# Row sums on one core: the first block loaded in one piece instead of four, and SyncE made to see the loads' ends before the store

## The chip, the cores and the metric

One core of one Trainium2 chip. VectorE (DVE) and ScalarE (ACT) do the sums; SyncE (SP in the views) issues every transfer, and 16 DMA engines carry it out in packets (before's records have 896 packets of 64 KB, 56 one behind the other on each of 16 engines). The metric is the device time of one execution in microseconds (us), lower is better. Every run quoted here is of the fast state, with a granted clock of 1.0. One kernel's executions differ by up to 0.7 us among themselves. Apart from one experiment (e3), the effects studied here are no larger than that, so times are compared within one set of runs on one chip, and the parts are read from traces, where most of them repeat far more closely.

## The reference

```python
x = np.random.randn(32, 512, 1024).astype(np.float32)      # 67.11 MB
out = (np.sum(x, axis=-1) * 0.5).astype(np.float32)         # 32 x 512
```

The 16,384 rows lie on 128 partitions, 128 rows each. They are worked in eight blocks of 16 rows per partition (8.39 MB a block).

## The kernel before

Seven whole blocks, then one cut in pieces. Three buffers; DVE sums one half of a block, ACT the other.

```python
for b in range(n_blocks - 1):
    t = x_pool.tile([P, B, D], fp32, name="xb")             # 3 buffers
    step = 4 if b == 0 else 1                               # block 0: four loads of 32 partitions,
    for q in range(step):                                   # every fourth partition each
        nc.sync.dma_start(out=t[q:P:step], in_=x_rows[q:P:step, c0 : c0 + B, :])
    # ... reduce_sum and a multiply on DVE for rows 0-7, act_row on ACT for rows 8-15
# last block: three loads of whole rows (8, 5, 2), two for the last row (640 and 384 columns)
# ... the last two DVE sums take the last row's two parts
nc.sync.dma_start(out=out_view, in_=res)                    # the store

def start_loads_at_entry(nc_):
    # moves SyncE's leading loads, up to the first that has to wait, in front of the entry barrier
    ...
```

Block 0's four loads are called strided quarters below. So before has 4 + 6 + 5 = 15 loads. The first six need no buffer to come free and are issued in front of the entry barrier, the point at which all engines wait for each other at the start. Each DMA counts on one of eight semaphores, which the program hands out in turn. The store is the 16th DMA and gets the eighth semaphore. At the end of the program SyncE waits once more for every semaphore and then enters the final barrier.

Of the kernel before, what the change touches and what calls it, by code (L numbers as in the profile page):

```python
# [1 line left out]

# [4 lines left out]


@with_exitstack
def kernel(  # L10
    ctx: ExitStack,
    tc: tile.TileContext,
    x: bass.AP,
    multiplier: float,
    out: bass.AP,
):







    nc = tc.nc
    P = nc.NUM_PARTITIONS
    fp32 = mybir.dt.float32
    ADD = mybir.AluOpType.add

    x_flat = x.flatten_outer_dims()
    N, D = x_flat.shape  # L30
    rows = N // P
    x_rows = x_flat.rearrange("(p c) d -> p c d", p=P)
    out_view = out.rearrange("b s -> (b s)").rearrange("(p c) -> p c", p=P)
    mul = float(multiplier)

    B = 16
    n_blocks = rows // B
    assert N == P * rows and rows == n_blocks * B

    x_pool = ctx.enter_context(tc.tile_pool(name="x", bufs=3))  # L40
    res_pool = ctx.enter_context(tc.tile_pool(name="res", bufs=1))
    sums = res_pool.tile([P, rows], fp32, name="sums")
    res = res_pool.tile([P, rows], fp32, name="res")
    part = res_pool.tile([P, 1], fp32, name="part")

    def act_row(t, r, col):
        nc.scalar.activation(  # L47
            out=t[:, r, :],
            in_=t[:, r, :],
            func=mybir.ActivationFunctionType.Copy,  # L50
            scale=mul,
            accum_out=res[:, col : col + 1],
        )

    def dve_span(t, r, lo, hi, dst, start=0.0):
        mid = (lo + hi) // 2
        nc.vector.tensor_tensor_reduce(  # L57
            out=t[:, r, lo:mid],
            in0=t[:, r, lo:mid],
            in1=t[:, r, mid:hi],  # L60
            scale=mul,
            scalar=start,
            op0=ADD,
            op1=ADD,
            accum_out=dst,
        )

    for b in range(n_blocks - 1):
        c0 = b * B
        t = x_pool.tile([P, B, D], fp32, name="xb")  # L70
        step = 4 if b == 0 else 1
        for q in range(step):
            nc.sync.dma_start(  # L73
                out=t[q:P:step], in_=x_rows[q:P:step, c0 : c0 + B, :]
            )
        h = B // 2
        nc.vector.reduce_sum(  # L77
            out=sums[:, c0 : c0 + h], in_=t[:, 0:h, :], axis=mybir.AxisListType.X
        )
        nc.vector.tensor_single_scalar(  # L80
            out=res[:, c0 : c0 + h],
            in_=sums[:, c0 : c0 + h],
            scalar=mul,
            op=mybir.AluOpType.mult,
        )
        for r in range(h, B):
            act_row(t, r, c0 + r)

    c0 = (n_blocks - 1) * B
    t = x_pool.tile([P, B, D], fp32, name="xb")  # L90
    cut = 640
    pieces = [(0, 8), (8, 13), (13, 15)]
    for lo, hi in pieces:
        nc.sync.dma_start(out=t[:, lo:hi, :], in_=x_rows[:, c0 + lo : c0 + hi, :])  # L94
    for lo, hi in ((0, cut), (cut, D)):
        nc.sync.dma_start(
            out=t[:, B - 1, lo:hi], in_=x_rows[:, c0 + B - 1, lo:hi]
        )
    on_act = {4, 5, 6, 7, 11, 12, 14}
    for r in range(B - 1):  # L100
        if r in on_act:
            act_row(t, r, c0 + r)
        else:
            dve_span(t, r, 0, D, res[:, c0 + r : c0 + r + 1])
    dve_span(t, B - 1, 0, cut, part)
    dve_span(t, B - 1, cut, D, res[:, rows - 1 : rows], start=part)

    nc.sync.dma_start(out=out_view, in_=res)

    def start_loads_at_entry(nc_):  # L110



        entry, *rest = nc_.main_func.blocks
        is_sp = lambda i: i.engine == mybir.EngineType.SP
        is_load = lambda i: type(i).__name__ == "InstDMACopy"
        for block in rest:
            body = list(block.instructions)
            own = [i for i in body if is_sp(i)]
            if not any(is_load(i) for i in own):  # L120
                continue
            lead = []
            for i in own:
                if not is_load(i) or i.sync_info.on_wait:
                    break
                lead.append(i)
            names = {i.name for i in lead}
            block.instructions = [i for i in body if i.name not in names]
            head = list(entry.instructions)
            at = next(  # L130
                k for k, i in enumerate(head) if is_sp(i) and type(i).__name__ == "InstDrain"
            )
            entry.instructions = head[:at] + lead + head[at:]
            return

    nc.at_finalize(start_loads_at_entry)


# [1 line left out]
_INS = ['x', 'multiplier']  # L140
_OUTS = [((32, 512), 'float32')]

_NUMBERS = {'multiplier': 0.5}


# [26 lines left out]
```

## Time and profile before

| | before |
|---|---|
| median of the runs | 163.25 us (163.19 to 163.28, 6 runs) |
| span of the profiled run | 161.62 us (that run took 163.42 us) |
| DVE, ACT busy | 68.1, 67.9 us (42% each) |
| data moved | 67.18 MB, 416 GB/s over the span |

The page of the kernel before: busy time; the rate of the DMA in 40 slices of the span; and the chain of waits that ended last, as shares of the span.

```profile
span 161.6 us, 242 instructions
...
DVE 68.1 (42%) x34; ACT 67.9 (42%) x127; POOL 0.2 (0%) x4
...
GB/s 260 519 373 406 519 373 405 519 389 389 519 357 422 519 389 389 519 405 373 519 422 359 519 438 341 519 438 341 519 438 341 519 438 341 430 438 398 424 375 28
...
DMA 85%; DVE 11%; SPq 2%; issue 0%; DVEq 0%
```

The chain is DMA for 85% of the span, and neither compute engine is busy for even half of it: the stream of loads bounds the kernel. The rate in a slice swings (519, 373, ...) because a packet's bytes are booked where the packet starts. A packet of a whole block is the 64 KB that one partition gets of it. In the trace's DMA records it takes 2.418 us on its engine, so 16 engines move 16 x 65,536 B / 2.418 us = 434 GB/s, and 67.11 MB need 154.8 us of the 161.6. Only the start and the end are left to save on. The first slice has 260 GB/s.

The windows view of before, first two stretches (columns: stretch in us, its length, busy time and count of DVE, ACT and POOL, clock, DMA share, GB/s); and SyncE's issues in front of the barrier in the timeline (start, length, engine, line).

```profile
0.00:2.00 2.00, 0.00 (x0) 0.00 (x0) 0.20 (x4) 1.00 0.73 262
2.00:4.00 2.00, 0.00 (x0) 0.00 (x0) 0.00 (x0) 1.00 0.67 262
```

```profile
0.00 3.74 SPq L73 DMA_DIRECT2D xb<-in_x_dram  x6
```

262 GB/s for 2 us are 0.52 MB, or eight packets of 64 KB, as many as start there in the records: by 2 us half of the 16 engines have started. Issuing the six loads takes SyncE 3.74 us; the trace puts the barrier's end at 4.06 us.

What SyncE waited for around the end (line, what it waited for, us in total, times, longest).

```profile
SPq L108 <- DVE res L57: 47.7, 1, 47.7
...
SPq L167 <- DMA out_dram<-res: 0.9, 1, 0.9
```

L108 is the store: it waits for the last DVE sum. L167 is the end of the program: 0.9 us until the store's landing is seen.

### The profile page before, as it was taken

The numbers are of one execution on the slowest core, as the hardware profiler recorded it, in microseconds if no ns is written. First come the engines' busy times: TensorE is split into PE (matmuls) and PEld (weight loads), VectorE is DVE, ScalarE is ACT, GpSimd is POOL, SyncE is SP. The second block draws the span as 40 slices with busy tenths as digits, with TensorE's granted clock in tenths as the row PEclk, the third lists the DMA queues.
The fourth block names the chain that finished last, engine by engine and source line by source line (L and its number), as shares of the span: only waits on it lengthen the run. The fifth ranks groups of instructions, "written<-read, shape, count | busy, mean of one in ns | idle before, by whom it ended". The sixth has DMA issues, their size and how long they took to land.

```text
span 161.6 us, 242 instructions
## 1 busy us (share of the span) xinstructions
DVE 68.1 (42%) x34; ACT 67.9 (42%) x127; POOL 0.2 (0%) x4
## 2 busy tenths in 40 slices
DVE  0000039800596007940099101990039800597453
ACT  0000039900595007920099101990039700596852
POOL 0000000000000000000000000000000000000000
DMA  6989989988989988998998997997997997999990
GB/s 260 519 373 406 519 373 405 519 389 389 519 357 422 519 389 389 519 405 373 519 422 359 519 438 341 519 438 341 519 438 341 519 438 341 430 438 398 424 375 28
DMA packets 1921, 67.18 MB, mean 416 GB/s; under 512 B 256, under 2 KB 512, under 8 KB 640
## 3 DMA queue, kind: packets, MB, share of 16 engines
q1 hardware_dynamic: 1920, 67.18, 96.7%
q14 instruction: 1, 0.01, 0.0%
HBM read 67.11 MB, written 0.07 MB: 416 GB/s over the span
## 4 chain that ended last, share of the span: by engine, by line
DMA 85%; DVE 11%; SPq 2%; issue 0%; DVEq 0%
DMA xb<-in_x_dram 85%; DVE sums L77 11%; SPq L73 2%; SPq L94 1%; DVE xb L57 1%; DVE part L57 0%; DVEq L167 0%
## 5 line engine op out<-in xcount | busy, mean ns | idle before, releaser
L77 DVE TENSOR_REDUCE sums<-xb 128x8 f32<-128x8192 f32 x7 | 60.8, 8686 | 85.7 <-DMA xb<-in_x_dram 85.7
L47 ACT ACTIVATE xb<-xb 128x1024 f32<-128x1024 f32 x63 | 65.6, 1043 | 67.8 <-DMA xb<-in_x_dram 67.8
L47 ACT ACTIVATION_READ_ACCUMULATOR xb<-xb 128x1 f32 x63 | 11.8, 187 | 0.0
L47 ACT ACT_TABLE_LOAD x1 | 1.3, 1283 | 22.8 <-DMA xb<-in_x_dram 22.8
L57 DVE CUSTOM_DVE_ANT_0 xb<-xb 128x512 f32<-128x512 f32 (+1 forms) x9 | 5.6, 667 | 5.1 <-DMA xb<-in_x_dram 4.9
L80 DVE TENSOR_SCALAR res<-sums 128x8 f32<-128x8 f32 x7 | 1.2, 172 | 0.2
L57 DVE DVE_READ_ACCUMULATOR2_ANT res<- 128x1 f32 x9 | 0.7, 83 | 0.0
L57 DVE CUSTOM_DVE_ANT_0 xb<-xb,part 128x192 f32<-128x192 f32 x1 | 0.4, 418 | 0.1
L153 POOL MEMSET const-bfloat16-1.0<- 128x1 bf16 x1 | 0.1, 102 | 0.0
L153 POOL MEMSET const-uint8-127<- 128x1 uint8 x1 | 0.1, 102 | 0.0
L153 POOL MEMSET const-float32-0.0<- 128x1 f32 x1 | 0.1, 99 | 0.2 <-issue 0.2
L153 POOL MEMSET const-float32-1.0<- 128x1 f32 x1 | 0.1, 99 | 0.0
L57 DVE DVE_READ_ACCUMULATOR2_ANT part<- 128x1 f32 x1 | 0.1, 81 | 0.0
## 6 DMA issues: line engine op xcount, KB each, us to landing
xb<-in_x_dram SPq DMA_DIRECT2D x1, 4096.0 KB, 39.6
xb<-in_x_dram SPq DMA_DIRECT2D x1, 2560.0 KB, 45.4
xb<-in_x_dram SPq DMA_DIRECT2D x1, 1024.0 KB, 47.4
xb<-in_x_dram SPq DMA_DIRECT2D x1, 320.0 KB, 47.7
xb<-in_x_dram SPq DMA_DIRECT2D x1, 192.0 KB, 47.6
xb<-in_x_dram SPq DMA_DIRECT2D x10, 43.8
out_dram<-res SPq DMA_DIRECT2D x1, 64.0 KB, 1.5
```

The costliest lines, as they stand in the source:

```text
L47: nc.scalar.activation(out=t[:, r, :], in_=t[:, r, :], func=mybir.ActivationFunctionType.Copy, scale=mul, accum_out=res[:, col : col + 1],)
L57: nc.vector.tensor_tensor_reduce(out=t[:, r, lo:mid], in0=t[:, r, lo:mid], in1=t[:, r, mid:hi], scale=mul, scalar=start, op0=ADD, op1=ADD, ...
L73: nc.sync.dma_start(out=t[q:P:step], in_=x_rows[q:P:step, c0 : c0 + B, :])
L77: nc.vector.reduce_sum(out=sums[:, c0 : c0 + h], in_=t[:, 0:h, :], axis=mybir.AxisListType.X)
L80: nc.vector.tensor_single_scalar(out=res[:, c0 : c0 + h], in_=sums[:, c0 : c0 + h], scalar=mul, op=mybir.AluOpType.mult,)
L94: nc.sync.dma_start(out=t[:, lo:hi, :], in_=x_rows[:, c0 + lo : c0 + hi, :])
L153: nc = _bacc.Bacc("TRN2", target_bir_lowering=False, num_devices=1)
```

## The change

Two things. Block 0 becomes one load of all 128 partitions, so that three loads (blocks 0 to 2) instead of six go in front of the barrier. And a no-op on SyncE, ahead of the store, depends on the last eight loads and the last ACT row, so that SyncE has seen their ends while DVE's last sum still runs.

```diff
+    loads = []
+    acts = []
 ...
-        step = 4 if b == 0 else 1
-        for q in range(step):
-            nc.sync.dma_start(
-                out=t[q:P:step], in_=x_rows[q:P:step, c0 : c0 + B, :]
-            )
+        loads.append(nc.sync.dma_start(out=t, in_=x_rows[:, c0 : c0 + B, :]))
 ...  (the other loads and the ACT rows are appended to the lists too)
-    nc.sync.dma_start(out=out_view, in_=res)
+    seen = nc.sync.nop()
+    for i in loads[-8:] + acts[-1:]:
+        tc.add_manual_dep(seen.ins, i.ins.name, ... reason="ends seen early")
+    store = nc.sync.dma_start(out=out_view, in_=res)
+    tc.add_manual_dep(store.ins, seen.ins.name, ... reason="in this order")
```

More of the change, by code (lines that the diff above doesn't have):

```diff
@@ L44 @@
     part = res_pool.tile([P, 1], fp32, name="part")
+    loads = []
+    acts = []
     def act_row(t, r, col):
-        nc.scalar.activation(
+        acts.append(nc.scalar.activation(
             out=t[:, r, :],
@@ L52, in act_row @@
             accum_out=res[:, col : col + 1],
-        )
+        ))
     def dve_span(t, r, lo, hi, dst, start=0.0):
@@ L70 @@
         t = x_pool.tile([P, B, D], fp32, name="xb")
-        step = 4 if b == 0 else 1
-        for q in range(step):
-            nc.sync.dma_start(
-                out=t[q:P:step], in_=x_rows[q:P:step, c0 : c0 + B, :]
-            )
+        loads.append(nc.sync.dma_start(out=t, in_=x_rows[:, c0 : c0 + B, :]))
         h = B // 2
@@ L93 @@
     for lo, hi in pieces:
-        nc.sync.dma_start(out=t[:, lo:hi, :], in_=x_rows[:, c0 + lo : c0 + hi, :])
+        loads.append(
+            nc.sync.dma_start(
+                out=t[:, lo:hi, :], in_=x_rows[:, c0 + lo : c0 + hi, :]
+            )
+        )
     for lo, hi in ((0, cut), (cut, D)):
-        nc.sync.dma_start(
-            out=t[:, B - 1, lo:hi], in_=x_rows[:, c0 + B - 1, lo:hi]
+        loads.append(
+            nc.sync.dma_start(
+                out=t[:, B - 1, lo:hi], in_=x_rows[:, c0 + B - 1, lo:hi]
+            )
         )
@@ L106 @@
     dve_span(t, B - 1, cut, D, res[:, rows - 1 : rows], start=part)
-    nc.sync.dma_start(out=out_view, in_=res)
+    seen = nc.sync.nop()
+    for i in loads[-8:] + acts[-1:]:
+        tc.add_manual_dep(
+            seen.ins,
+            i.ins.name,
+            mybir.DependencyInfo(mybir.DependencyClass.Sync, mybir.DependencyReason.DATA),
+            reason="ends seen early",
+        )
+    store = nc.sync.dma_start(out=out_view, in_=res)
+    tc.add_manual_dep(
+        store.ins,
+        seen.ins.name,
+        mybir.DependencyInfo(mybir.DependencyClass.NoSync, mybir.DependencyReason.SCHED_ONLY),
+        reason="in this order",
+    )
     def start_loads_at_entry(nc_):
```

## The prediction

> **What bounds the kernel now.** The stream of loads. The profile's page has DVE and ACT busy for 42% of the span each, the chain of waits is 85% DMA, and the windows view shows 431 to 434 GB/s from 24 to 120 us. In the trace's DMA records every 64 KB packet takes 2.418 us on its engine, which is 16 x 65,536 B / 2.418 us = 434 GB/s; 67.11 MB at that rate need 154.8 us. The span is 161.6 us, so everything else is worth 6.8 us: about 1.4 to 2.7 us until each engine's first packet starts, about 0.4 us because the first packets are slow (2.4 to 3.2 us), the slow small pieces and the unequal ends of the 16 engines (157.3 to 158.2 us), then the tail.
>
> **What the change does.**
>
> 1. Head. The first block comes as one 8.39 MB load of 128 partitions instead of four of 32. SyncE issues three loads in front of the barrier instead of six. The six issues take 3.74 us (timeline, SyncE); three should take about 1.7 us (0.54 to 0.76 each at the start, 0.33 alone later). The entry barrier moves from 4.07 to near 2.1 us, off the critical path: DVE and ACT wait for block 0, of which the last part is seen at 22.8 us. An earlier first compute is off the path too: block 3 is issued at 32.6 us, and the queue holds work until 61 us.
>    What matters is only when the 16 engines start their streams. [...] four quarters give each engine eight packets, as one load would[...]. The first engine starts 1.36 us after the first issue. The final store, also 128 partitions, starts moving 0.85 us after its issue, with all engines within 0.2 us. So a 128-partition issue need not start later than a quarter; a smaller stagger could save up to 0.7 us, a slower issue cost 0.3. Middle: 0.1 us saved.
>
> 2. Tail. The last sum ends at 159.19 us. SyncE then runs one semaphore wait (159.21) and the store's issue (159.26). With the other ends seen by a no-op while the sum runs (last load's end seen at 158.65, ACT done at 158.51, about 55 ns per further wait), only DVE's semaphore is left and the store can issue at once: 0.05 us saved. After the store's issue SyncE runs four waits for loads, 159.66 to 159.87; these hide behind the store's flight (landing seen at 160.82), so removing them gives nothing. If the wait pair after the landing shrinks to the final drain alone, another 0.06 us.
>
> **Sum.** 163.19 - 0.1 - 0.1 = 163.0 us.
>
> **What would show it.** The entry issues end near 1.7 us; DMA share from 4 us on unchanged; last load landing 157.6 to 158.4 us after the start; store issued under 50 ns after DVE's last instruction (75 ns now); landing-to-end about 0.75 us.
>
> **What would make it wrong.** The first 128-partition issue delaying all engines by over 0.5 us, or first packets colliding longer; a stagger at the start that vanishes (gain near 1 us); the no-op's waits ordered so that they end after the last sum, delaying the store by 0.1 to 0.3 us.

The 0.1 us at the head and its bounds of 0.7 and 0.3 us are estimates.

## The result, and the profile after

| | before | after |
|---|---|---|
| median | 163.25 us | 162.93 us (162.86 to 163.16, 6 runs) |
| ratio, 95% interval | | 0.9984 [0.9971, 0.9996] |
| span of the profiled run | 161.62 us | 161.14 us (that run took 162.93 us) |

A ratio is the mean time of one kernel's fast runs over that of the other's of the same rounds, so it is not quite the ratio of the medians. The change saves about 0.3 us, 0.2%. The two profiled spans differ by 0.48 us, more than the medians do, because the profiled run of before was itself 0.17 us above its median.

The page after, the same lines:

```profile
span 161.1 us, 233 instructions
...
DVE 68.1 (42%) x34; ACT 67.9 (42%) x127; POOL 0.2 (0%) x4
...
GB/s 260 521 456 325 521 456 325 521 456 325 521 456 325 521 456 325 521 439 342 521 439 344 521 423 358 521 423 358 521 407 374 521 407 374 415 439 411 423 381 30
...
DMA 86%; DVE 11%; SPq 1%; issue 0%; DVEq 0%
```

Work and bound are the same. The first slice, about 4 us wide, again has 260 GB/s (16 packets start in it), so the difference has to be looked for inside it: the windows view and the issues after.

```profile
0.00:2.00 2.00, 0.00 (x0) 0.28 (x1) 0.20 (x4) 1.00 1.39 492
2.00:4.00 2.00, 0.00 (x0) 1.01 (x1) 0.00 (x0) 1.00 0.08 33
```

```profile
0.00 1.32 SPq L74 DMA_DIRECT2D xb<-in_x_dram  x3
```

492 GB/s for 2 us are 15 packets: by 2 us all engines but one have started, where before it was eight. This count wanders from trace to trace (12 in e2, which starts as before does, and 11 in e10, which is the changed kernel again), so the experiments below go by the engines' third packets. Three issues take 1.32 us, and the barrier is passed at 1.65 us. That ACT's 1.28 us table load now comes at once (the 0.28 and 1.01 us) changes nothing, since block 0 lands after 22 us.

SyncE's waits around the end, after:

```profile
SPq L115 <- DMA xb<-in_x_dram: 47.2, 2, 38.9
...
SPq L188 <- DMA out_dram<-res: 1.2, 1, 1.2
...
SPq L123 <- DVE res L60: 0.4, 1, 0.4
```

L115 is the no-op: the wait that the store had now lies there, and 0.4 us are left for the store (L123). The wait for the landing (L188) grew from 0.9 to 1.2 us only because SyncE arrives at it sooner.

What that is worth shows in SyncE's own instructions, from the trace's records (start in us; the semaphores waited for are in brackets, 105 in before and 102 in after being DVE's, 104 and 101 ACT's, the rest the DMAs'; before's store counts on 108, after's on 105):

```
                               before                     after
last DVE instruction ends      159.185                    158.683
waits in front of the store    159.213 [105]              158.711 [102, 99]
store issued                   159.259 [104]              158.776 [101]
waits while it flies           159.659 [102]              -
                               159.713 [103, 101]
                               159.774 [106, 100]
                               159.839 [107, 99]
landing seen                   160.824 [108, 105]         160.350 [105]
last wait                      160.889 [104]              160.404 [102]
enters the final barrier       160.948                    160.463
```

From the last DVE instruction to the store's issue: 0.074 us before, 0.093 after. From the landing seen to the barrier: 0.124 before, 0.113 after. Beside before, then, the tail brought nothing (+0.019 - 0.011 us), and the whole 0.5 us between these two traces was there when DVE's last sum began. That looks as if the no-op were useless. The experiments show otherwise.

### The profile page after: what moved, and what is told of

The parts are those of the page before. It is cut to its first block, busy times and chain, and to the rows that moved or that the text cites. A ratio compares the mean times of both kernels' runs of the same rounds, so it can differ in the third digit from the quotient of the medians.

```text
span 161.1 us, 233 instructions
## 1 busy us (share of the span) xinstructions
DVE 68.1 (42%) x34; ACT 67.9 (42%) x127; POOL 0.2 (0%) x4
## 4 chain that ended last, share of the span: by engine, by line
DMA 86%; DVE 11%; SPq 1%; issue 0%; DVEq 0%
DMA xb<-in_x_dram 86%; DVE sums L76 11%; SPq L94 1%; DVE xb L60 1%; SPq L74 0%; DVE part L60 0%; DVEq L188 0%
```

## The experiments

All gave correct results. The first set of four, the second and the third each ran on a chip of its own with its own runs of before (medians 163.27, 163.29 and 163.21 us). "Last load packet" is when the slowest DMA engine finished its share of the last load; "landing to barrier" is from the store's landing seen by SyncE to its entry into the final barrier. Both come from the records of the one profiled run. "Third packet" is the mean start of the 16 engines' third packets: by then the start-up is over, and they run at about 2.42 us a packet (e3's at 5.11).

| run | first issue, us | third packet, us | last load packet, us | landing to barrier, us | median, us | ratio to before |
|---|---|---|---|---|---|---|
| before | 0.542 | 7.27 | 158.18 | 0.124 | 163.25 | |
| after | 0.377 | 6.98 | 157.68 | 0.113 | 162.93 | 0.9984 |
| e1, head only | 0.377 | 6.98 | 157.70 | 0.310 | 163.23 | 1.0001 |
| e2, no-op only | 0.547 | 7.27 | 158.21 | 0.112 | 163.45 | 1.0009 |
| e3, quarters in blocks | 0.371 | 11.10 | 178.32 | 0.124 | 183.69 | 1.1251 |
| e4, whole, then quarters | 0.374 | 6.90 | 157.71 | 0.123 | 162.96 | 0.9984 |
| e5, quarters by rows | 0.377 | other packets | 157.71 | 0.124 | 162.92 | 0.9972 |
| e6, one in front | 0.369 | 6.93 | 157.97 | 0.113 | 163.09 | 0.9982 |
| e7, head only, last semaphore | 0.361 | 6.95 | 157.76 | 0.124 | 163.24 | 0.9997 |
| e8, before, first semaphore | 0.542 | 7.23 | 158.34 | 0.354 | 163.79 | 1.0028 |
| e10, after again | 0.369 | 6.95 | 157.72 | 0.112 | 162.96 | 0.9980 |
| e11, head only again | 0.371 | 6.89 | 157.64 | 0.311 | 163.15 | 0.9994 |
| e12, no-op only again | 0.542 | 7.25 | 158.00 | 0.113 | 163.24 | 0.9999 |
| e9, none in front | 0.370 | 6.89 | 157.74 | 0.113 | 163.61 | 1.0022 |

Times in a trace count from the first load's issue. For e9 alone that is 0.731 us after the span's start.

The theory: all of the gain is at the head, and the no-op is worth nothing. The rival: part of it comes from the tail.

### e1_head_only

```diff
-    seen = nc.sync.nop()
-    for i in loads[-8:] + acts[-1:]: ...
-    store = nc.sync.dma_start(out=out_view, in_=res)
+    nc.sync.dma_start(out=out_view, in_=res)
```

> The changed kernel without the no-op. Theory (all of the gain is at the head; the tail's change is worth nothing): the same time as the changed kernel, 162.9 us, ratio to before 0.998; last sum to store's issue 0.07 us. Rival (the no-op at the tail brings part of it): nearer to before, 163.1 us or more. First issue about 0.38 us long, first packet near 1.14 us, last load packet near 157.7 us.

163.23 us, ratio 1.0001 [0.9989, 1.0013]: no gain that the runs show, although the loads end as early as after the change (157.70 us). The theory fell. The trace says where it went:

```
e1: store issued 158.781, counts on 105
    159.180 [104]                    one wait while it flies
    160.349 [105, 103]               landing seen
    160.410 [106, 100]
    160.474 [107, 99]
    160.536 [108, 102]
    160.601 [101]
    160.659                          enters the final barrier: 0.310 us after the landing
```

With 12 loads the store is the 13th DMA and gets the fifth semaphore, 105, which stands second in the final list, the fixed list of waits at the end of the program. SyncE takes the list in order, so three more pairs of waits, long fulfilled, run after the landing at about 62 ns each. Before, with 15 loads, the store had the last DMA semaphore of the list, and those waits ran during its flight. The head's change thus moved waits onto the critical path, and the no-op, after which the final list holds only the store and DVE, takes them off again.

The profile's view of waits for e1 has the same wait for the landing and nothing of the pairs behind it, because a wait that is already fulfilled is no wait; one has to read the instructions:

```profile
SPq L115 <- DVE res L60: 47.8, 1, 47.8
SPq L174 <- DMA out_dram<-res: 1.1, 1, 1.1
```

### e2_tail_only

```diff
-        loads.append(nc.sync.dma_start(out=t, in_=x_rows[:, c0 : c0 + B, :]))
+        step = 4 if b == 0 else 1
+        for q in range(step):
+            loads.append(nc.sync.dma_start(out=t[q:P:step], in_=x_rows[q:P:step, c0 : c0 + B, :]))
```

> The kernel before (four strided quarters) with the no-op at the end. Theory: the same as before, 163.25 us, within 0.05; last sum to store's issue about 0.09 us, as the store still has two waits of its own. Rival (tail brings 0.1 us or more): 163.1 us or less. It also gives a second trace of the head of before: first issue about 0.54 us, first packet 1.36 us.

163.45 us, ratio 1.0009 [0.9997, 1.0021]. The no-op alone gives nothing: landing to barrier 0.112 us against 0.124, and the store is issued 0.093 us after the last DVE instruction against 0.074. The median lies 0.2 above the expected one; the repetition (e12) did not confirm that as an effect.

### e3_quarters_in_blocks

No no-op, and:

```diff
-        loads.append(nc.sync.dma_start(out=t, in_=x_rows[:, c0 : c0 + B, :]))
+        n = 4 if b == 0 else 1
+        for q in range(n):
+            p0, p1 = q * P // n, (q + 1) * P // n
+            loads.append(nc.sync.dma_start(out=t[p0:p1], in_=x_rows[p0:p1, c0 : c0 + B, :]))
```

> No no-op; the first block in four quarters of 32 neighbouring partitions instead of every fourth. If the stride of four is what makes the first issue longer: as the changed kernel, first issue 0.38 us, 162.9 us. If the count of issues or the 32 partitions are: as before, 0.54 us, 163.2 us.

The first issue is 0.371 us, as expected if the stride makes it long. But the time is 183.69 us, 12.5% slower, which neither expectation had. The page of e3, first slices:

```profile
span 181.8 us, 242 instructions
...
DMA  9999998859999899999997999999989999899991
GB/s 231 231 231 231 231 231 173 173 115 462 462 404 404 375 433 462 462 462 462 447 404 346 418 463 462 462 462 447 404 375 389 462 462 462 346 462 396 433 386 69
```

The windows view of before and of e3, a stretch of each while loads stream (the last two columns are DMA share and GB/s):

```profile
24.00:40.00 16.00, 7.73 (x2) 8.54 (x17) 0.00 (x0) 1.00 1.00 434
```

```profile
10.00:20.00 10.00, 0.00 (x0) 0.00 (x0) 0.00 (x0) 1.00 1.02 210
```

For the first nine slices, block 0, the DMA engines are as busy as ever (a DMA share of 1.02 in the stretch above, 1.00 in before's) and move half as much (210 GB/s against 434): a 64 KB packet of block 0 takes 5.11 us (median), one of the later blocks 2.42. Why 32 neighbouring partitions halved the rate is not shown here. Every fourth partition from 0 to 127 did not: before's strided quarters run at 2.418 us a packet. So of the two ways to cut by partitions tried here, only the strided one of before keeps the rate. The slow block hides what the first issue is worth, so e3 decides nothing about the time of the start.

### e4_full_then_quarters

```diff
-        step = 4 if b == 0 else 1        # of e2, without the no-op
+        step = 4 if b == 1 else 1
```

> No no-op; the first block in one load, the second in four strided quarters: six issues in front of the barrier again, but the first is a whole one. If the first issue alone sets when the engines start: as the changed kernel, 162.9 us, first packet 1.14 us. If the six issues in a row disturb the start, or the barrier at about 4 us counts: as before, 163.2 us.

162.96 us, ratio 0.9984 [0.9971, 0.9997]: the whole gain. Six issues are in front of the barrier, which is passed at 4.28 us, later than before's 4.06. So neither the number of issues in front nor the barrier's time counts, and four strided quarters do no harm in second place. What counts is the first issue. The stride makes an issue longer in second place too: the first of these strided issues takes 0.535 us, where the second whole one after the change takes 0.424. This kernel has 15 loads, so its store is last in the list (0.123 us) and needs no no-op: with the same start as e1 and another place in the list, its mean time is 0.25 us lower, with a 95% interval of 0.27 either way (worked out from the six runs of each).

### e5_quarters_by_rows

No no-op, and:

```diff
-        loads.append(nc.sync.dma_start(out=t, in_=x_rows[:, c0 : c0 + B, :]))
+        n = 4 if b == 0 else 1
+        for q in range(n):
+            r0, r1 = q * B // n, (q + 1) * B // n
+            loads.append(nc.sync.dma_start(out=t[:, r0:r1, :], in_=x_rows[:, c0 + r0 : c0 + r1, :]))
```

> No no-op; the first block in four loads of four rows each, every one of all 128 partitions: the same number of issues in front of the barrier as before (six), 15 loads in all, so the store gets the last of the eight semaphores. If it is the strided partitions of the first issue that start the engines late: like the changed kernel, first issue 0.38 us, last load packet 157.7 us, 162.95 us. If splitting the first block in four does it: like before, 158.2 us and 163.25 us.

162.92 us, ratio 0.9972 [0.9956, 0.9988], and 157.71 us as with one load. Cutting block 0 in four costs nothing that these runs show when each part has all 128 partitions; it is the strided first part that starts the engines late. Like e4, this kernel gets the store's place in the list for free. Its interval overlaps that of the changed kernel, so it is as good and not shown to be better.

### e7_head_only_last_lane

```diff
-        loads.append(nc.sync.dma_start(out=t, in_=x_rows[:, c0 : c0 + B, :]))   # of e1
+        n = 2 if b in (3, 4, 5) else 1       # two halves by rows
+        ...
```

> The changed head, no no-op, and three blocks in the middle loaded as two halves each, only so that the store gets the last of the eight semaphores instead of the fifth. Theory (without the no-op, waits listed after the store's semaphore in the final list run after its landing, about 62 ns each): landing seen to the last drain falls from 0.31 to about 0.12 us, time 163.0 us, 0.2 below the head-only kernel. Rival (the no-op does something else, or the 0.3 us of the head-only kernel was noise): no change, 163.2 us, or landing to drain still 0.3 us.

In the trace exactly as the theory has it: landing to barrier falls from 0.310 to 0.124 us with no no-op, only because the store stands elsewhere in the list. In time it missed: 163.24 us, ratio 0.9997 [0.9981, 1.0014], where 163.0 was expected; the rival had 163.2. Its five runs go from 162.98 to 163.56 us, and the profiled one is the fastest. So the runs of e7 don't confirm what the place in the list is worth in time. One cause may be the halves: e7 and e8 both cut blocks in the middle, and both took some 0.2 us more than expected, while e5, on the same chip and with only block 0 cut, did not. That the halves cost it is not shown.

### e8_before_first_lane

```diff
         step = 4 if b == 0 else 1            # of before
+        n = 2 if b in (3, 4, 5, 6) else 1    # each load in n halves by rows
+        ...
```

> The kernel before, with four blocks in the middle loaded as two halves each, so that the store gets the first semaphore of the final list instead of the last. Theory: four more wait pairs run after the landing, landing to the last drain rises from 0.12 to about 0.37 us, time about 0.25 us over before, 163.5 us. Rival: no change.

Landing to barrier rises from 0.124 to 0.354 us: 0.23 us for four pairs, as expected. The time rises by 0.50 us (163.79 against 163.29; ratio 1.0028 [1.0015, 1.0042]), twice as much. In the trace, the last load packet comes at 158.34 us, 0.16 later than in before's; why isn't explained here.

### e6_one_in_front

```diff
                 lead.append(i)
+                if len(lead) == 1:
+                    break
```

> The changed kernel with only the first load in front of the barrier, the other two behind it. Theory (only the first issue's start matters, an engine has 19 us of work from it): the same as the changed kernel, 162.9 us. Rival (three in front are needed): slower by up to the 0.5 us of the barrier.

163.09 us, ratio 0.9982 [0.9969, 0.9996]; the changed kernel's is 0.9984. One load in front is as good as three, as far as these runs can tell. The last load packet of its profiled run was at 157.97 us, though its third packets (6.93 us) were as early as the others': the end of the stream wanders by some 0.3 us from run to run.

### e10_after_again, e11_head_only_again, e12_tail_only_again

The changed kernel, e1 and e2 once more, side by side on one chip.

> The changed kernel as it is, for a comparison on one chip with the two that follow. 162.95 us, ratio to before 0.998; landing to last drain 0.11 us; last load packet 157.7 us.

> The changed kernel without the no-op, again. Theory: 0.20 us over the changed kernel (three more waits after the landing), 163.15 us; landing to last drain 0.31 us. Rival: equal to it.

> The strided quarters with the no-op, again: differs from the changed kernel only in the first block's load. Theory: 0.3 to 0.5 us over the changed kernel, 163.3 to 163.4 us, equal to before; first issue 0.54 us, last load packet 158.2 us, landing to last drain 0.11 us.

162.96, 163.15 and 163.24 us, with before at 163.21. Without the no-op: 0.19 us more, where the traces give 0.311 - 0.112 = 0.20. Without the new head: 0.28 us more, where the third packets are 7.25 - 6.95 = 0.30 us later; just under the range of 0.3 to 0.5 that was expected. Against before, the head alone has 0.9994 [0.9980, 1.0008], the no-op alone 0.9999 [0.9984, 1.0014], both together 0.9980 [0.9965, 0.9995]. Only the pair is clear of 1. Set directly against each other, the five runs of each have a mean 0.23 us higher without the no-op (95% interval 0.02 to 0.44) and 0.30 us higher without the new head (0.11 to 0.50): both halves count, and neither size is known from times to better than 0.2 us. That the traces give the same sizes is what makes them credible.

### e9_none_in_front

```diff
-    def start_loads_at_entry(nc_): ...
-    nc.at_finalize(start_loads_at_entry)
```

> The changed kernel with no load in front of the barrier. The barrier is passed at 0.69 us where one issue of 0.37 us lies in front of it, so with none at about 0.5 us; all loads start that much later: 0.4 to 0.6 us over the changed kernel, about 163.4 us. It tells what having a load in front is worth at all, beside which three or six is small.

163.61 us, 0.65 over the changed kernel on the same chip, just over the expected range. The barrier is passed at 0.65 us, where 0.5 was expected, the first load is issued at 0.731 us, and the rest is as after the change. So moving a load in front of the barrier is worth 0.65 us, and before and after both have that.

## Why the prediction was right

163.0 us was predicted, 162.93 measured. The total is right because two terms of the sum were mis-sized in opposite directions: the head, forecast at -0.1 us, brought about -0.3, and the tail, forecast at -0.1, brought nothing beside before. That they cancelled is luck. Of the saving, 0.19 us were forecast and 0.25 to 0.32 measured.

- **What bounds the kernel, and what does not matter.** Right. The stream bounds it before and after; the barrier moved from 4.06 to 1.65 us (2.1 predicted) and the issues end at 1.32 us (1.7 predicted) without effect. e4, with the barrier at 4.28 us, and e6, at 0.69 us, are as fast as the change.
- **"Middle: 0.1 us saved" at the head.** Mis-sized: about 0.3 us. The third packets start at 7.23 to 7.27 us in the four traces that begin with a strided quarter and at 6.89 to 6.98 in the seven others with whole 64 KB packets that have a load in front of the barrier and no blocked quarters (after, e1, e4, e6, e7, e10, e11); e12 against e10 gives 0.28 us of time. The prediction left room for a stagger of up to 0.7. Its ground for the small middle was that the 128-partition store starts moving 0.85 us after its issue, "so a 128-partition issue need not start later than a quarter". It starts earlier: the first issue takes 0.36 to 0.38 us instead of 0.54 to 0.55, and the first packet comes at 1.00 to 1.14 us instead of 1.33 to 1.36. The trace of before could not show that the stride is to blame: its first issue could as well have been long for being the first, and the whole loads issued behind the quarters took 0.58 and 0.46 us. The issue's length does not cover the movement of the data here: after the change the first issue takes 0.377 us, and the end of its load is seen at 22.4 us. The first issue is about 0.17 us shorter, and the first packet follows its end after 0.63 to 0.76 us instead of 0.78 to 0.81. Together that is about the size of the 0.3, but no run takes the two apart, and why the stride makes the issue longer stays open.
- **"only DVE's semaphore is left and the store can issue at once: 0.05 us saved".** Wrong. One load's semaphore (99) was left over to the store's own waits beside DVE's, and the store kept its wait for ACT, although the no-op had waited for ACT too. The store is issued 0.093 us after the last DVE instruction, 0.019 later than before.
- **"If the wait pair after the landing shrinks ... another 0.06 us".** Wrong: a wait for the landing and one for DVE remain, 0.113 us instead of 0.124.
- **"these hide behind the store's flight, so removing them gives nothing".** True of before, and wrong as a judgement of the no-op. The step that failed was to take the final list as given while the other half of the change alters it. Fewer loads put the store on the fifth semaphore instead of the eighth, and 0.19 us of waits would have run after the landing. That eats most of the head's gain: e1, the head alone, is not measurably faster than before. The final list is made of instructions that only wait, most of them for two semaphores, and here each took about 62 ns. What that costs depends on where in the list the last semaphore to be fulfilled stands: here 0.124 us from the landing to the barrier with the store's standing last (e7), 0.310 second (e1), 0.354 first (e8).
- **"four quarters give each engine eight packets, as one load would".** The traces of before and after show that, and the prediction set four quarters equal to one load. That holds for the rate of the strided quarters (2.418 us a packet) and not in general: e3's blocks keep all the engines busy too (a DMA share of 1.02) and run at half the rate (5.11 us a packet).

In sum: head about -0.3 us, store's place in the list +0.19, no-op -0.19, store's issue +0.02. That makes -0.3, and 0.25 to 0.32 us were measured.

## What to carry to other kernels

When loads bound a kernel, look at how the very first one is issued: here a plain load of all 128 partitions started as soon as any (first packet at 1.00 to 1.14 us, against 1.33 to 1.36 for a strided quarter), cutting it by rows cost nothing that the runs show (ratio to before 0.9972 in e5, 0.9984 for the change), and blocks of 32 neighbouring partitions halved the rate (5.11 us a packet against 2.418). Waits that were already fulfilled were not free here (about 62 ns an instruction), and which of them run after the last landing depended on where the store's semaphore stood in the final list, which the number of DMAs changed (0.124 us from the landing to the barrier when it stood last, 0.354 when first); so read the instructions behind the last landing, and don't trust the view of waits there. And when a change has two halves, ask what one does to the other before calling one of them worthless.
